# Differential attention written in a fixed, skewed order of units, with output-projection pieces as filling

## The chip, the cores and the metric

One core of one Trainium2 chip. The metric is the device time of one execution in microseconds (us), the median of three runs.

## What is computed

A decoder trunk of two layers on x of 1024 rows by 1024 columns, float32. Each layer first mixes tokens in three groups (a gated convolution A, differential attention B, a chunked gating unit C), projects the joined result with `w_out`, and then runs a convolutional feed-forward part. Shifts, scales and gates ("modulation") come from a conditioning vector through `w_ada`. The part that the change touches is B, here for head h and the 128 query rows of block i (cut from the reference):

```python
for i in range(seq // ATTN_BLOCK):
    q0 = i * ATTN_BLOCK
    end = q0 + ATTN_BLOCK
    qb, kb, vb = q[:, :, :, q0:end], k[:, :, :, :end], v[:, :, :end]   # 2 maps m per head, 64 columns each
    s = jnp.einsum("bhmqd,bhmkd->bhmqk", qb, kb) * scale
    mask = jnp.arange(end)[None, :] <= (q0 + jnp.arange(ATTN_BLOCK))[:, None]
    p = jax.nn.softmax(jnp.where(mask, s, -jnp.inf), axis=-1)
    a = p[:, :, 0] - lam * p[:, :, 1]
    outs.append(jnp.einsum("bhqk,bhke->bhqe", a, vb))
o = rms_norm(concatenate(outs), subln_g) * (1.0 - lam_init)
```

## The kernel before

TensorE (PE) does the matmuls, VectorE (DVE) and ScalarE (ACT) what lies between them, GpSimd (POOL) some of the weight preparation; SyncE (SP) issues all DMAs. Products of float32 precision are three matmuls of split operands: names that end in `h` and `l` are the high and low part of a matrix.

A layer runs in this order. Stage 1 projects the input: the gated convolution, v, the gating unit (stage C, with the tiles `zc`, `uv`, `cvh`, `cvl`, `sv`), then q and k of the heads. The taps of the convolution (`convacc`) and, in layer 0, the modulation (`macc`, `modp`: a weighted sum on DVE of eight `w_ada` tiles, one multiply each, for each of six columns) run beside the projections as background. Then comes attention, then the boundary (matmuls `og`, the rest of the output projection), then the feed-forward part.

Attention has 4 heads of 8 row blocks, 32 units. Block i sees i+1 blocks of keys, so a unit is `w = (i+1)*128` wide. A unit is:

- scores `sc` of maps m=0 and 1 on PE (`score`, L733, on 64 rows each; the mask is added by a matmul, L735). If i >= 4 each map has its own score slot in PSUM of 1024 columns; if i < 4 both share one. There are two slots.
- the maximum `mx` on DVE (one for each map if i >= 4, L754, otherwise one for both, L756), the exponential `p` with its sum on ACT (L759)
- reciprocal, `rho` and the difference of the maps on DVE (L762 to L767)
- transposes `at` on PE (L774) and their copies on ACT (L775), the product with v, `pv`, on PE (L778), its scaling `ot` and sum of squares on ACT (L780, L781)

`head_end` normalises a head, turns it and splits it into `ybh`, `ybL`, which are the left operands of a part of the output projection.

Beside the units runs filling: `out_fill` computes the output projection in pieces of 512 columns, `of`. First 16 pieces over four contraction blocks (12 matmuls each, from `yah`, `ych` and the split weights `woh`, `wol`), then 16 pieces over two blocks (6 matmuls each, from heads 0 and 1). Each ends with a sum into the residual tile `r` on DVE (L862). During attention PSUM holds the two score slots, three banks for `at`, `pv` and the like, and one bank, `fill`, for the pieces and for the key projection of head 3 (`prf`). A scheduler sets the order on each engine: attention is a generator and the pieces are recorded after it, and the scheduler moves them between the units. Weights for the pieces are loaded, multiplied by the gate row on POOL (`scaled_wout`, L682) and split by a copy on ACT and a subtraction (`split_wout`).

In layer 0 the modulation of column 3 runs within attention from head 1 on, one step after each unit; its page holds three raw tiles `wada` and the sum.

Of the kernel before, what the change touches and what calls it, by code (L numbers as in the profile page):

```python
# [50 lines left out]
class Trunk:  # L51
# [575 lines left out]
    def stage1(self, l, H, O, pre):  # L627
# [7 lines left out]
        if l == 0:  # L635
            self.mod_cfg = ("Rb", "Rb")
            self.bg.append(self.mix(self.mods(0, (2, 4)), self.conv_taps(l, self.y[0], self.acc[0], 0)))
        else:
            self.bg.append(self.conv_taps(l, self.y[0], self.acc[0], 0))
# [24 lines left out]
        self.at = O + "c"  # L664
        att = self.attention(l, self.X, O, stk, vp, grow)
        self.qk_head(l, 3, H, O, 0, (0,))
        next(att)
        self.qk_head(l, 3, H, O, 0, (1,), True)
        self.at = self.X + "c"
        return att, grow  # L670
# [66 lines left out]
    def attn_unit(self, l, at, stk, vp, i, ot, ss):  # L737
        nc = self.nc
        w = (i + 1) * P
        small = i < 4  # L740
        sums = self.sm("sums", [P, 2], bufs=4)
        mx = self.sm("mx", [P, 2], bufs=4)
        if small:
            ps2 = self.mm("sc")
            p2 = self.page("tmp", "p")
            ps = [ps2[:, 0:512], ps2[:, 512:1024]]
            pr = [p2[:, 0:512], p2[:, 512:1024]]
        else:
            ps = [self.mm("sc"), self.mm("sc")]
            pr = [self.page("tmp", "p") for _ in range(2)]  # L750
        self.score(ps, stk, i)
        for m in range(2):
            if not small:
                nc.vector.tensor_reduce(out=mx[:, m:m + 1], in_=ps[m][:, :w], axis=AX.X, op=ALU.max, negate=True)  # L754
        if small:
            nc.vector.tensor_reduce(out=mx, in_=ps2.rearrange("p (m k) -> p m k", m=2)[:, :, :w], axis=AX.X,  # L756
                                    op=ALU.max, negate=True)
        for m in range(2):
            nc.scalar.activation(out=pr[m][:, :w], in_=ps[m][:, :w], func=AF.Exp, bias=mx[:, m:m + 1],  # L759
                                 accum_out=sums[:, m:m + 1])  # L760
        rc = self.sm("rc", [P, 2], bufs=4)
# [4 lines left out]
        ad = pr[0]  # L766
        self.unit_end = nc.vector.scalar_tensor_tensor(out=ad[:, :w], in0=pr[1][:, :w], scalar=rho, in1=ad[:, :w],  # L767
                                       op0=ALU.mult, op1=ALU.add)
        a = self.page(at, "at")
        for b0 in range(0, i + 1, 4):  # L770
            b1 = min(i + 1, b0 + 4)
            pb = self.bank("at")
            for j in range(b0, b1):
                nc.tensor.transpose(pb[:, (j - b0) * P:(j - b0 + 1) * P], ad[:, j * P:(j + 1) * P], self.ident)  # L774
            nc.scalar.copy(a[:, b0 * P:b1 * P], pb[:, :(b1 - b0) * P])  # L775
        po = self.bank("pv")
        for j in range(i + 1):
            nc.tensor.matmul(po[:, 0:P], a[:, j * P:(j + 1) * P], vp[:, j, :], start=j == 0, stop=j == i)  # L778
        o = ot[:, i, :]
        nc.scalar.activation(out=o, in_=po[:, 0:P], func=AF.Identity, scale=rc[:, 0:1])  # L780
        nc.scalar.activation(out=po[:, 256:384], in_=o, func=AF.Square, accum_out=ss[:, i:i + 1])  # L781

    def head_end(self, l, h, O, ot, ss, halves=(0, 1)):
# [3 lines left out]
        self.rsqrt(ss[:, cs], ss[:, cs])  # L787
        o = ot[:, cs]
        nc.vector.tensor_tensor(out=o, in0=o, in1=ss[:, cs].unsqueeze(2).to_broadcast([P, 4 * len(halves), P]),
                                op=ALU.mult)  # L790
# [25 lines left out]
    def attention(self, l, H, O, stk, vp, grow):  # L816
        pend = None
        for h in range(4):
            ot = self.page("rows", "ot", shape=(P, NT, P))
            ss = self.sm("oss", [P, NT])  # L820
            for n, i in enumerate((7, 6, 3, 5, 2, 4, 1, 0) if h < 3 else (7, 6, 5, 4, 0, 1, 2, 3)):
                self.attn_unit(l, self.at, stk, vp, i, ot, ss)
                if n == 1 and pend:
                    self.head_end(*pend)
                if h >= 1 and l == 0:
                    if n == 0 and h == 1:
                        self.mod_cfg = (None, None)
                        mt = self.page(H + "a", "wada", shape=(P, 4, 1024))
                        self.mod_tile = [mt[:, i] for i in range(4)]
                        late = self.mods(0, (3,))  # L830
                    with self.tc.issue_after(self.unit_end.ins):
                        next(late, None)
                if n == (1 if h else 4) and h + 1 < 4:
                    nxt = self.load_stacks(l, h + 1, H)
                    nvp = self.load_vp(l, h + 1)
                k = {(2, 3): 0, (2, 5): 1, (2, 7): 2, (3, 0): 3}.get((h, n))
                if k is not None:
                    if k < 2:
                        self.lhs0.append(self.load_yb(l, k, O))
                    self.wB.append(self.load_wout(l, 2 + k, O, grow, self.page(O + "a", "wout")))  # L840
                if h == 3 and n == 4:
                    self.head_end(l, h, O, ot, ss, (1,))
                yield
            pend = (l, h, O, ot, ss)
            stk, vp = nxt, nvp
        self.head_end(*pend, (0,))
        if l == 0:
            for _ in late:
                pass
            self.affine_cols(0, 1)  # L850

    def out_fill(self, lhs, w, r, tiles, scale=1.0):
        nc = self.nc
        for t in tiles:
            ts_ = slice(t * P, (t + 1) * P)
            for n in range(2):
                ns = slice(n * 512, (n + 1) * 512)
                pb = self.bank("of", "fill")
                for k in range(len(lhs)):
                    self.mm3(pb, lhs[k][0][:, ts_], lhs[k][1][:, ts_], w[k][0][:, ns], w[k][1][:, ns], k == 0,  # L860
                             k == len(lhs) - 1)
                nc.vector.scalar_tensor_tensor(out=r[t][:, ns], in0=r[t][:, ns], scalar=scale, in1=pb, op0=ALU.mult,  # L862
                                               op1=ALU.add)
# [26 lines left out]

    def stage3(self, l, H, O, att):
        nc = self.nc
        att, grow = att
        raws = self.page(H + "a", "wout", shape=(P, 4, 1024))
        for i in range(4 - len(self.woA)):
            self.woA.append(self.scaled_wout(l, KA[len(self.woA)], grow, raws[:, i]))
        wA = [self.split_wout(O, raw) for raw in self.woA]
        ab = None
        if l == 0:
            ab = self.page("rows", "ab")  # L900
# [530 lines left out]
```

## Time and profile before

| | before |
|---|---|
| median of three runs | 2440.6 us (2437.98 to 2442.28) |
| profiled execution: time, span | 2437.79 us, 2436.1 us |
| PE, DVE, ACT, POOL busy | 2308.1, 1956.1, 1049.9, 328.9 us |
| granted PE clock, mean | 0.974 |
| attention, layer 0 (286.0 to 507.1) | 221.1 us |
| attention, layer 1 (1492.0 to 1708.2) | 216.2 us |
| stage C to the end of `sv`, layer 0 and 1 | 86.7 and 75.4 us |

The profiled execution is one run of the program; its span ends a little before its time does. Times in the trace count from the start of the span. A matmul's row has a modelled end, so the time that a run of matmuls takes is read from the start of the first to the start of what follows.

### The profile page before, as it was taken

What the parts mean: (1) busy time and instruction counts of PE and PEld (TensorE: products, weight loads), DVE (VectorE), ACT (ScalarE), POOL (GpSimd) and SP (SyncE); (2) the same over time, 40 slices, a digit from 0 to 9 for tenths busy, and PEclk for the clock granted to TensorE, in tenths of its full rate; (3) what the DMA queues carried; (4) which work ended last, traced back from release to release, by engine and by line L of the source; (5) the groups of instructions that cost most, each with busy time, mean ns of one, the idle gap of its engine ahead of it and who ended that gap; (6) DMA issues with size and microseconds to landing.
All of it is one profiled execution on the core that took longest, in us unless ns stands there. A gap on an engine that the chain in (4) does not pass through costs nothing.

```text
span 2436.1 us, 28260 instructions
## 1 busy us (share of the span) xinstructions
PE 2308.1 (95%) x10846; PEld 1886.4 (77%) x10846; DVE 1956.1 (80%) x2650; ACT 1049.9 (43%) x1692; POOL 328.9 (13%) x165
## 2 busy tenths in 40 slices
PE   8998999979999999999959999999899999999996
PEld 7787778767888887788848877777688888878885
DVE  7898876778887888877978988657987777797857
ACT  4214754646554555311130257555654555561111
POOL 1143260410000000000020541214100000000003
PEclk9998999999999999999979999999999999999998
DMA  7433462122332333745523244320232222254301
GB/s 294 156 116 120 140 224 104 61 95 90 110 113 88 112 113 121 263 141 179 190 70 117 78 143 160 130 95 27 99 100 87 78 78 87 87 176 169 122 26 69
DMA packets 87672, 294.06 MB, mean 121 GB/s; under 512 B 9265, under 2 KB 18801, under 8 KB 86001
## 3 DMA queue, kind: packets, MB, share of 16 engines
q1 hardware_dynamic: 87536, 292.26, 35.4%
q8 instruction: 85, 1.39, 0.2%
q14 instruction: 51, 0.41, 0.1%
HBM read 228.23 MB, written 64.00 MB: 120 GB/s over the span
## 4 chain that ended last, share of the span: by engine, by line
PE 67%; DVE 17%; issue 6%; ACT 4%; DMA 3%; POOL 2%; SPq 0%; POOLq 0%; DVEq 0%; ACTq 0%
PE upb L1083 6%; PE upb L1084 6%; PE upb L1085 6%; PE og L130 5%; PE og L131 5%; PE og L132 5%; PE sc L733 3%; PE upd L1084 3%; PE upd L1085 3%; PE upd L1083 3%; DVE convacc L410 2%; PE pv L778 2%; PE of L130 2%; PE of L132 2%; PE of L131 2%
## 5 line engine op out<-in xcount | busy, mean ns | idle before, releaser
L1083 PE MATMUL upb<-comb,uw 128*128 128x512 f32 x704 | 274.9, 391 | 9.9 <-DVE upc L1107 5.0
L130 PE MATMUL og<-dn,dn 128*128 128x512 f32 x704 | 275.3, 391 | 2.6 <-ACT r L885 2.1
L131 PE MATMUL og<-dn,dn 128*128 128x512 f32 x704 | 274.5, 390 | 0.0
L132 PE MATMUL og<-dn,dn 128*128 128x512 f32 x704 | 274.3, 390 | 0.0
L1084 PE MATMUL upb<-comb,uw 128*128 128x512 f32 x704 | 274.0, 389 | 0.0
L1085 PE MATMUL upb<-comb,uw 128*128 128x512 f32 x704 | 273.9, 389 | 0.0
L1107 DVE TENSOR_TENSOR uw<-wu,uw 128x512 fp32r<-128x512 f32 x210 | 144.1, 686 | 125.3 <-ACT uw L1110 125.3
L1120 DVE SCALAR_TENSOR_TENSOR cv<-upc,pc,cv 128x1023 f32<-128x1023 f32 (+1 forms) x176 | 225.4, 1280 | 2.9
L138 POOL TENSOR_TENSOR lnrs<-lnrs,mhalf 128x1 f32<-128x1 f32 x32 | 24.8, 779 | 1421.4 <-DVE lnrs L137 1414.9
L887 DVE TENSOR_TENSOR r<-og,r 128x1024 f32<-128x1024 f32 x128 | 155.7, 1218 | 59.0 <-PE og L132 58.4
L410 DVE SCALAR_TENSOR_TENSOR convacc<-convy,pc,convacc 128x1023 f32<-128x1023 f32 (+14 forms) x120 | 176.2, 1469 | 2.3
L125 ACT CAST dn<-actr 128x1024 fp32r<-128x1024 f32 x44 | 46.1, 1049 | 298.1 <-issue 224.4
L1083 PEld LDWEIGHTS upb<-comb,uw 128*128 128x128 f32 x704 | 132.1, 188 | 41.0 <-DVE upc L1107 6.7
L1110 ACT CAST uw<-wu 128x512 fp32r<-128x512 f32 x210 | 121.7, 616 | 83.6 <-DVE wu L1107 77.1
L130 PEld LDWEIGHTS og<-dn,dn 128*128 128x128 f32 x704 | 132.2, 188 | 31.5 <-ACT r L885 3.4
L1085 PEld LDWEIGHTS upb<-comb,uw 128*128 128x128 f32 x704 | 132.2, 188 | 27.5
L132 PEld LDWEIGHTS og<-dn,dn 128*128 128x128 f32 x704 | 132.2, 188 | 27.4
L1084 PEld LDWEIGHTS upb<-comb,uw 128*128 128x128 f32 x704 | 132.2, 188 | 27.2
L131 PEld LDWEIGHTS og<-dn,dn 128*128 128x128 f32 x704 | 132.2, 188 | 26.8
L1083 PE MATMUL upd<-comb,uw 128*128 128x512 f32 x352 | 137.3, 390 | 0.0
L1085 PE MATMUL upd<-comb,uw 128*128 128x512 f32 x352 | 136.9, 389 | 0.0
L1084 PE MATMUL upd<-comb,uw 128*128 128x512 f32 x352 | 136.9, 389 | 0.0
(312 smaller groups left out, 5474.4 us busy)
## 6 DMA issues: line engine op xcount, KB each, us to landing
wada<-in_w_ada SPq DMA_DIRECT2D x96, 512.0 KB, 4.6
wu<-in_w_up_t SPq DMA_DIRECT2D x84, 512.0 KB, 3.6
d_act<-cv SPq DMA_DIRECT2D x44, 512.0 KB, 2.6
actr<-d_act SPq DMA_DIRECT2D x44, 512.0 KB, 4.6
wdn<-in_w_down SPq DMA_DIRECT2D x44, 512.0 KB, 4.2
win<-in_w_fm SPq DMA_DIRECT2D x24, 512.0 KB, 4.0
wtm<-in_w_tm SPq DMA_DIRECT2D x16, 512.0 KB, 3.7
wout<-in_w_out SPq DMA_DIRECT2D x16, 512.0 KB, 6.2
```

Of the source, the lines that this page charges most:

```text
L130: mm(ps, lh, rh, start=first, stop=False)
L131: mm(ps, lh, rl, start=False, stop=False)
L132: mm(ps, ll, rh, start=False, stop=last)
L410: nc.vector.scalar_tensor_tensor(out=acc[:, d:], in0=y[:, :S - d], scalar=w(30 - d), in1=acc[:, d:], op0=ALU.mult, op1=ALU.add)
L733: nc.tensor.matmul(ps[m][:, c0:c1], q[ms, isl], k[ms, c0:c1], start=n == 0, stop=n == 2 and c1 != w)
L887: nc.vector.tensor_tensor(out=r[t], in0=ps, in1=r[t], op=ALU.add)
L1083: mm(ps, w[:, 0, ks], hi[k], start=k == 0 and not more, stop=False, skip_group_check=True)
L1084: mm(ps, w[:, 0, ks], lo[k], start=False, stop=False, skip_group_check=True)
L1085: mm(ps, w[:, 1, ks], hi[k], start=False, stop=k == 3, skip_group_check=True)
L1107: v.tensor_tensor(out=o, in0=x, in1=y, op=op)
L1110: act.copy(self.up_w[n][:, 0], src)
L1120: v.scalar_tensor_tensor(out=u[:, d:], in0=c[:, :S - d], scalar=self.ffw[:, 2 - d, m:m + 1], in1=u[:, d:], op0=ALU.mult, op1=ALU.add)
```

## The change

Attention no longer depends on the scheduler: it stands in a section in which PE, ACT and DVE keep the order of the code. The unit is cut into `att_score`, `att_max`, `att_exp`, `att_diff`, `att_turn`, `att_copy`, `att_mix` and `att_out`, and three units are in flight: in step g stand the scores, maxima and exponentials of unit g, the difference, transposes and copies of unit g-1, and the product and scaling of unit g-2. `ev` is the residual sum of a filling piece; it is issued one step after its piece, behind the maxima of the next unit.

```diff
-            self.bg.append(self.mix(self.mods(0, (2, 4)), ...))
+            self.bg.append(self.mix(self.mods(0, (2,)), ...))
...
+        with self.tc.manual_schedule(engines={nc.tensor.engine, nc.scalar.engine, nc.vector.engine}):
+            r = self.attention(l, H, self.X, O, stk, vp, grow, wk)
...
+        for g, (h, n, i) in enumerate(units):
...
+            self.att_score(u, stk)
+            if one:
+                self.att_diff(l, one)
+            self.att_max(u)
+            if one:
+                self.att_turn(one)
+            self.att_exp(u)
+            if one:
+                self.att_copy(one, (O if g < 7 else X) + "c")
+            if ev:
+                ev()
+            if two:
+                self.att_mix(two)
+            fills = keys if g < 8 else fillA if g < 22 else fill0
+            ev = next(fills, None) if g < 4 or 10 <= g < 21 or g >= 26 else None
+            if two:
+                self.att_out(two)
...
+            if 10 <= g < 15 or g >= 26:
+                if ev:
+                    ev()
+                ev = next(fills, None)
...
+            k = {4: 0, 5: 1, 8: 2, 9: 3}.get(g)
+            if k is not None:
+                self.wA.append(self.split_wout(O, self.woA[k]))
...
+            if h == 1 and n == 3 and l == 0:
+                self.mod_cfg = (None, None)
+                self.mod_tile = [self.page(X + "c", "wada") for _ in range(2)]
+                late = self.mods(0, (3, 4))
...
+            if g == 21:
...
+                wr = [self.scaled_wout(l, 2 + k, grow, self.page(O + "a", "wout")) for k in range(2)]
+            if g in (23, 24):
...
+                self.wB.append(self.split_wout(O, wr[g - 23]))
+            if g == 25:
+                wr = [self.scaled_wout(l, 4 + k, grow, self.page(O + "a", "wout")) for k in range(2)]
+            if g in (28, 29):
+                self.wB.append(self.split_wout(O, wr[g - 28]))
+            next(late, None)
+            one, two = u, one
```

The blocks of head 0 come in the order 3, 7, 6, 2, 5, 1, 4, 0, of heads 1 and 2 in 7, 6, 3, 5, 2, 4, 1, 0 and of head 3 in 7, 6, 5, 4, 0, 1, 2, 3, as before but for head 0. The key projection of head 3 is cut into four chunks of 12 matmuls for g = 0 to 3 (evacuated on ACT, `evac`, one step after the second and the fourth) and three steps of its rotation. The 16 long pieces stand two in each unit of g = 10 to 14 and one in g = 15 to 20, the short ones two in each unit from g = 26 and four behind the last. `head_end` is cut into `head_norm`, `head_scale` and `head_turn`. The modulation of column 4 moves from stage 1 into attention, behind column 3, and their page has one raw tile and the sum. After the last unit its difference, transposes, product and scaling follow, and the four short pieces, each with its sum.

PE around a unit with i=5 of a later head, before. `sc` with two numbers is a score slot, `of` a piece, `at` and `pv` the transposes and the product with v.

```order
L774 MATMUL at_511_3038<-ident_69,p_506_3012 128x128 x4
L774 MATMUL at_512_3044<-ident_69,p_506_3012 128x128 x4
L733 MATMUL sc_544_3182<-stk_438_2770,stq_437_2768 128x512 x3
L733 MATMUL sc_544_3182<-stk_438_2770,stq_437_2768 128x256 x3
L735 LDWEIGHTS identb_74
L735 MATMUL sc_544_3182<-maskb_76,identb_74 128x128
L130 MATMUL of_717_3935<-woh_315_2320,yah_282_2106 128x512
L131 MATMUL of_717_3935<-wol_316_2321,yah_282_2106 128x512
```

And a unit with i=5 of the changed kernel:

```order
L735 MATMUL sc_427_2741<-stk_367_2514,stq_366_2512 128x256
L735 MATMUL sc_428_2742<-stk_367_2514,stq_366_2512 128x256
L735 MATMUL sc_427_2741<-stk_367_2514,stq_366_2512 128x256
L735 MATMUL sc_428_2742<-stk_367_2514,stq_366_2512 128x256
L737 LDWEIGHTS identb_74
L737 MATMUL sc_427_2741<-maskb_76,identb_74 128x128
L737 LDWEIGHTS identb_74
L737 MATMUL sc_428_2742<-maskb_76,identb_74 128x128
L792 MATMUL at_432_2765<-ident_69,p_420_2690 128x128 x4
L804 MATMUL pv_437_2778<-vp_368_2516,at_422_2694 128x128 x7
L131 MATMUL of_438_2786<-woh_341_2418,yah_272_2071 128x512
L132 MATMUL of_438_2786<-wol_342_2419,yah_272_2071 128x512
```

Before, the slot of one map is filled alone, with a piece behind it; now the two slots alternate, and transposes, product and piece stand behind both.

DVE in layer 0 before, where a head's units with i=7 and i=6 follow each other (`r` is the residual tile that a piece is summed into):

```order
L764 TENSOR_SCALAR rho_509_3034<-rc_508_3032,sums_502_3008,nlam0_103 128x1
L862 SCALAR_TENSOR_TENSOR r_385_2569<-r_385_2569,of_715_3907 128x512
L767 SCALAR_TENSOR_TENSOR p_506_3012<-p_507_3013,rho_509_3034,p_506_3012 128x1024
L754 TENSOR_REDUCE mx_516_3072<-sc_517_3073 128x1
L754 TENSOR_REDUCE mx_516_3072<-sc_518_3074 128x1
L862 SCALAR_TENSOR_TENSOR r_395_2602<-r_395_2602,of_716_3921 128x512
```

And in the changed kernel, for two units with i >= 4:

```order
L748 TENSOR_REDUCE mx_502_3126<-sc_498_3105 128x1
L748 TENSOR_REDUCE mx_502_3126<-sc_499_3106 128x1
L917 SCALAR_TENSOR_TENSOR r_458_2903<-r_458_2903,of_495_3086 128x512
L261 SCALAR_TENSOR_TENSOR wada_442_2820<-wada_441_2819,cact_85,wada_442_2820 128x1024
L777 RECIPROCAL rc_512_3175<-sums_506_3133 128x2
L779 TENSOR_SCALAR rho_513_3177<-rc_512_3175,sums_506_3133,nlam0_103 128x1
L782 SCALAR_TENSOR_TENSOR p_504_3131<-p_505_3132,rho_513_3177,p_504_3131 128x1024
L748 TENSOR_REDUCE mx_514_3180<-sc_510_3159 128x1
L748 TENSOR_REDUCE mx_514_3180<-sc_511_3160 128x1
L917 SCALAR_TENSOR_TENSOR r_458_2903<-r_458_2903,of_509_3142 128x512
```

The sum of a piece now always stands behind both maxima of the next unit, and a multiply of the modulation (`wada`) behind the sum.

DVE in stage C of layer 0 before, with the taps of the convolution and the multiplies of the modulation:

```order
L410 SCALAR_TENSOR_TENSOR convacc_150_1095<-convy_149_1093,pc0_89,convacc_150_1095 128x1003
L260 SCALAR_TENSOR_TENSOR macc_131_876<-wada_139_950,cact_85,macc_131_876 128x1024
L137 TENSOR_SCALAR crs_189_1362<-cmv_187_1356 128x2
L410 SCALAR_TENSOR_TENSOR convacc_150_1095<-convy_149_1093,pc0_89,convacc_150_1095 128x1002
L555 TENSOR_TENSOR zc_191_1423<-ptm_190_1374,brow_155_1109 128x1024
L260 SCALAR_TENSOR_TENSOR macc_131_876<-wada_140_954,cact_85,macc_131_876 128x1024
```

And DVE at the same taps in the changed kernel:

```order
L411 SCALAR_TENSOR_TENSOR convacc_140_1060<-convy_139_1058,pc0_89,convacc_140_1060 128x1002
L138 TENSOR_SCALAR crs_179_1327<-cmv_177_1321 128x2
L411 SCALAR_TENSOR_TENSOR convacc_140_1060<-convy_139_1058,pc0_89,convacc_140_1060 128x1001
L570 TENSOR_SCALAR uv_176_1319<-uv_176_1319,cmv_177_1321,crs_179_1327 128x256 x2
L411 SCALAR_TENSOR_TENSOR convacc_140_1060<-convy_139_1058,pc0_89,convacc_140_1060 128x1000
```

The multiplies (`macc`) between the taps are gone there.

More of the change, by code (lines that the diff above doesn't have):

```diff
@@ L747, in attn_unit @@
-            pr = [p2[:, 0:512], p2[:, 512:1024]]
-        else:
-            ps = [self.mm("sc"), self.mm("sc")]
-            pr = [self.page("tmp", "p") for _ in range(2)]
-        self.score(ps, stk, i)
+            pr = u["p"] = [p2[:, 0:512], p2[:, 512:1024]]
+        else:
+            pr = u["p"] = [self.page("tmp", "p") for _ in range(2)]
+        sums = u["sums"] = self.sm("sums", [P, 2], bufs=4)
         for m in range(2):
-            if not small:
-                nc.vector.tensor_reduce(out=mx[:, m:m + 1], in_=ps[m][:, :w], axis=AX.X, op=ALU.max, negate=True)
@@ L755, in attn_unit, with att_diff @@
[L755 to L759, printed above, removed]
+            nc.scalar.activation(out=pr[m][:, :w], in_=u["ps"][m][:, :w], func=AF.Exp, bias=u["mx"][:, m:m + 1],
                                  accum_out=sums[:, m:m + 1])
[L761 removed]
+    def att_diff(self, l, u):
+        nc = self.nc
+        w, sums = u["w"], u["sums"]
+        rc = u["rc"] = self.sm("rc", [P, 2], bufs=4)
@@ L765, in attn_unit, with att_turn @@
                                 op1=ALU.mult)
[L766 to L769, printed above, removed]
+        ad = u["p"][0]
+        nc.vector.scalar_tensor_tensor(out=ad[:, :w], in0=u["p"][1][:, :w], scalar=rho, in1=ad[:, :w], op0=ALU.mult,
+                                       op1=ALU.add)
+    def att_turn(self, u):
+        i, ad = u["i"], u["p"][0]
+        u["pb"] = []
         for b0 in range(0, i + 1, 4):
@@ L814, in load_yb @@
         return hi, lo
[L816 to L846, printed above, removed]
@@ new lines, in key_chunks, with evac @@
+    def key_chunks(self, l, h, H, w):
+        nc = self.nc
+        m = ZT["k"] + h
+        hi, lo = w
+        bias = self.col(l, "bin", m)
+        z, rot = self.page("raw", "z"), self.page("Rb", "rot")
+        for half in range(2):
+            sl = slice(half * 512, (half + 1) * 512)
+            pb = self.bank("prf", "fill")
+            for k in range(KT):
+                ks = slice(k * P, (k + 1) * P)
+                self.mm3(pb, hi[:, ks], lo[:, ks], H[0][k][:, sl], H[1][k][:, sl], k == 0, k == KT - 1)
+                if k == 3:
+                    yield
+            def evac(sl=sl, pb=pb):
+                nc.scalar.activation(out=z[:, sl], in_=pb, func=AF.Identity, bias=bias)
+                self.rotate(rot[:, sl], pb, bias, 1.0)
+            yield evac
+        nc.vector.tensor_tensor(out=z, in0=z, in1=self.trig[0], op=ALU.mult)
+        yield
+        nc.vector.tensor_tensor(out=rot, in0=rot, in1=self.trig[1], op=ALU.mult)
+        yield
+        nc.vector.tensor_tensor(out=z, in0=z, in1=rot, op=ALU.add)
+        nc.scalar.copy(rot.bitcast(F32R), z)
+        nc.vector.tensor_tensor(out=z, in0=z, in1=rot, op=ALU.subtract)
+        for x, t in enumerate((rot, z)):
+            nc.sync.dma_start(self.d_k[l][h, :, x, :], t)
+        yield
@@ L889, in out_group @@
                 after(t)
[L891 to L900, printed above, removed]
-            nc.sync.dma_start(ab, self.gab(0, 0, 1))
-        order = (4, 5, 0, 1, 2, 3, 6, 7)
-        r = {}
-        for t in order:
-            next(att)
-            r[t] = self.load_res(t, ab)
-        for _ in att:
-            pass
-        self.out_fill(self.lhsA, wA, r, order, 1.0 if l else ALPHA)
-        self.out_fill(self.lhs0, self.wB[:2], r, order)
-        self.psum(3, 2)
-        self.up_first(l, O + "c")
-        return r, self.lhsB, self.wB[2:]
     def boundary(self, l, w, lhs, wts, r, X):
```

176 lines of the change are left out of this document (138 added, 38 removed).

## The prediction

> **What bounds the kernel now.** I read the share of each engine first, then the busy time in stretches (each layer's attention whole, then the four heads of layer 1), then the waits in that window.
>
> ```profile
> PE 2308.1 (95%) x10846; PEld 1886.4 (77%) x10846; DVE 1956.1 (80%) x2650; ACT 1049.9 (43%) x1692; POOL 328.9 (13%) x165
> ```
> ```profile
> core 0: us, PE busy (x) PEld busy (x) DVE busy (x) ACT busy (x) POOL busy (x), PEclk, DMA share, GB/s
> 286.00:507.10 221.10, 206.52 (x1170) 162.89 (x1170) 156.71 (x221) 125.07 (x317) 75.32 (x31) 0.95 0.33 115
> 1492.00:1708.20 216.20, 202.89 (x1153) 158.80 (x1153) 141.83 (x210) 124.96 (x318) 54.20 (x23) 0.97 0.27 98
> ...
> 1492.00:1549.00 57.00, 49.41 (x245) 37.42 (x244) 41.78 (x47) 42.40 (x80) 21.75 (x8) 0.88 0.58 216
> 1549.00:1601.00 52.00, 52.00 (x303) 41.03 (x303) 27.81 (x47) 23.46 (x70) 1.65 (x1) 1.00 0.15 52
> 1601.00:1647.00 46.00, 46.00 (x288) 37.33 (x287) 27.08 (x42) 26.14 (x74) 8.79 (x5) 1.00 0.28 97
> 1647.00:1708.00 61.00, 55.28 (x321) 42.84 (x321) 45.11 (x74) 32.83 (x95) 22.03 (x10) 1.00 0.09 27
> ```
> The kernel is bound by PE. Attention, which the change rewrites, takes 221.1 and 216.2 us. In heads 1 and 2 of layer 1 PE is never idle, while DVE is busy 53% and 59% of the time: whatever order the scheduler found there, it hides every maximum, exponential and residual sum under matmuls. Slack lies only in head 0 (7.6 us idle, clock 0.88) and at the end of head 3.
>
> ```profile
> PE of L130 <- DVE r L862: 5.2, 6, 1.8
> PE of L132 <- POOL yal L126: 3.6, 1, 3.6
> PE sc L733 <- ACT rot L380: 2.9, 1, 2.9
> PE sc L733 <- ACT p L759: 0.8, 2, 0.4
> ```
> So PE waits hardly at all for softmax (0.8 us), and for the sum of the previous filling piece six times. That wait exists because all pieces share one bank: the next one starts when the sum L862 has read the last. A new order can gain what PE does needlessly, and can lose all of this cover.
>
> **What PE does needlessly.** The rows below are PE in head 1 of layer 1.
>
> ```profile
> 1558.37 1.50 PE L733 MATMUL sc<-stk,stq 64*128 64x512 f32 x6
> 1559.80 0.23 PE L735 MATMUL sc<-maskb,identb 128*128 128x128 bf16 x1
> 1559.84 0.48 PE L130 MATMUL of<-woh,yah 128*128 128x512 f32 x1
> ...
> 1562.66 0.60 PE L778 MATMUL pv<-vp,at 128*128 128x128 f32 x4
> 1563.10 0.27 PE L774 MATMUL at<-ident,p 128*128 128x128 f32 x1
> 1563.30 0.97 PE L733 MATMUL sc<-stk,stq 64*128 64x512 f32 x6
> 1564.21 0.28 PE L735 MATMUL sc<-maskb,identb 128*128 128x128 bf16 x2
> ```
> Six score matmuls of one map, each on 64 rows, start over 1559.80 - 1558.37 = 1.43 us. Six of a small unit, whose two maps alternate on rows 0-63 and 64-127, take 1564.21 - 1563.30 = 0.91. The new order alternates in large units too. For i=7 (12 of these and 12 slots of 512 in two maps) the score falls from 2 x 1.43 to 2 x 0.91 us. With the narrower second halves in proportion, I estimate S = 1.8, 1.65, 1.5 and 1.4 us for i = 7, 6, 5, 4, against 3.0, 2.6, 2.3 and 2.2: 3.8 us a head, 15 us a layer. For i = 3, 2, 1, 0 S is about 1.1, 0.95, 0.8 and 0.75, as before. That is the only work saved.
>
> **What the order puts in the path.** Unit g now issues on PE: score(g), transposes of g-1, product with v of g-2, one filling piece; on DVE: difference of g-1, maxima of g, sum of the *previous* piece. The piece must wait for that sum, the sum stands behind both maxima, the maxima wait for the whole alternating score.
>
> ```profile
> L754 DVE TENSOR_REDUCE mx<-sc 128x1 f32<-128x1024 f32 x8 | 9.8, 1219 | 6.0 <-PE sc L735 6.0
> ...
> L754 DVE TENSOR_REDUCE mx<-sc 128x1 f32<-128x896 f32 x8 | 8.6, 1088 | 5.0 <-PE sc L735 5.0
> ...
> L759 ACT ACTIVATE p<-sc,mx 128x1024 f32<-128x1024 f32 x8 | 8.9, 1118 | 7.3 <-DVE mx L754 7.3
> ...
> L754 DVE TENSOR_REDUCE mx<-sc 128x1 f32<-128x768 f32 x8 | 7.6, 953 | 1.3 <-PE sc L735 1.2
> ...
> L754 DVE TENSOR_REDUCE mx<-sc 128x1 f32<-128x640 f32 x8 | 6.6, 822 | 6.8 <-PE sc L735 6.5
> ...
> L767 DVE SCALAR_TENSOR_TENSOR p<-p,rho,p 128x1024 f32<-128x1024 f32 x4 | 6.0, 1509 | 0.1
> ```
> ```profile
> 1696.97 0.50 PE L130 MATMUL of<-woh,ybh 128*128 128x512 f32 x1 [1.83 <-DVE r L862]
> ...
> 1698.23 0.39 PE L132 MATMUL of<-woh,ybL 128*128 128x512 f32 x1
> 1698.66 0.69 DVE L862 SCALAR_TENSOR_TENSOR r<-r,of 128x512 f32<-128x512 f32 x1 [1.06 <-PE of L132]
> ...
> 1699.40 0.19 PEld L130 LDWEIGHTS of<-woh,ybh 128*128 128x128 f32 x1 [1.21 <-DVE r L862]
> ```
> The second fence is the wait itself: 1.83 us where a normalisation stood before the sum on DVE; then last start at 1698.23, sum at 1698.66 for 0.69, next piece at 1699.40. From the last start that is 1.17 us, 0.94 of it without a start. A piece of twelve matmuls is 1562.66 - 1559.84 = 2.8 us, one of six 1.45.
>
> One piece in a large unit: S + two maxima + sum 0.69 + hand-overs 0.3 + piece 2.8. For i = 7, 6, 5, 4: 1.8 + 2.44 + 3.8 = 8.0; 7.6; 7.2; 6.8. Between score and piece PE has only the transposes and the product, about 0.11 us a matmul (the row of four at 1562.66 lasts to 1563.10): i=7 has 3.4 us to cover and 1.7 us of work, so 1.7 idle in each. A small unit has one maximum over both maps (1.22, 0.95, 0.69, 0.42 by the rows of the same widths, the last three estimated in proportion): i = 3, 2: 6.1, 5.6 us.
>
> Two pieces: add 0.94 + 2.8 (or 0.94 + 1.45). No piece: the next large unit needs both score slots, so it waits for the second exponential: S + two maxima + exponential 1.1 + 0.3: 5.7 for i=7, 5.2 for i=6; i = 4, 1, 0 give about 4.2, 3, 2.6.
>
> Now by head, layer 1. Head 0 has no output pieces, the key projection in their place, which must be evacuated from that bank by ACT; I take 57, as now (my bounds are 52 and 62: its two pieces, 5.7 us, leave it, and an evacuation on ACT stands ahead of the second half). Head 1: two units without piece, five with two long ones (i = 3, 5, 2, 4, 1), one with one: 5.7 + 5.2 + (9.8 + 10.9 + 9.3 + 10.5 + 9.0) + 5 = 65, against 52. Head 2: five units with one piece, three without: 8.0 + 7.6 + 6.1 + 7.2 + 5.6 + 9.8 = 44, against 46. Head 3: two without, six with two short pieces, then four short ones that have nothing but the sums beside them, and the last unit's way through difference (1.5 at most), transposes, copy, product and evacuation, 4.8 in all by my estimate: 10.9 + (8.2 + 7.8 + 6 + 6.3 + 6.7 + 7.2) + 4 x 2.44 + 4.8 = 68, against 61. In all +13 -2 +7 = +18 a layer, although PE does 15 us less. I use it for layer 0 too; the 5 us by which that is longer now stay in it. The split of `head_end` in three is costed at nothing: the same instructions, beside pieces that PE runs for 2.8 us; without that cover they would cost their 0.7 to 1.3 us each.
>
> Weight copies: `wout` loads at g=21 are scaled on POOL and copied by ACT at g=23 and 24, in its queue ahead of the next copies and exponentials. From load to scaled copy go 6.2 + 2.76 us, g=22 and 23 are about 6 us long.
>
> ```profile
> L682 POOL TENSOR_TENSOR wout<-wout,grow 128x1024 f32<-128x1024 f32 x6 | 16.5, 2763 | 19.5 <-DMA wout<-in_w_out 19.4 <-PE sc L735 0.2
> ```
> ```profile
> wada<-in_w_ada SPq DMA_DIRECT2D x96, 512.0 KB, 4.6
> ...
> wout<-in_w_out SPq DMA_DIRECT2D x16, 512.0 KB, 6.2
> ```
> I add 4 us a layer for it (0 to 8). Those at g=8, 9, 28 and 29 are older when copied: nothing.
>
> **Layer 0: the modulation.** Eight multiplies leave stage 1 and join eight others in attention, one per unit from g=11, with one raw page instead of three: each load starts after the multiply before it.
>
> ```profile
> L260 DVE SCALAR_TENSOR_TENSOR macc<-wada,cact,macc x7: 1272/1274/2308, 175.9 to 199.0; 128x1024 f32<-128x1024 f32 x7
> L258 DVE TENSOR_SCALAR macc<-wada,cact x1: 710/710/710, 172.8 to 172.8; 128x1024 f32<-128x1024 f32 x1
> ```
> ```profile
> 139.20:225.90 86.70, 79.66 (x347) 64.99 (x345) 83.75 (x106) 18.40 (x20) 34.33 (x16) 0.92 0.30 99
> 1357.10:1432.50 75.40, 71.67 (x328) 59.39 (x326) 70.76 (x90) 18.71 (x21) 37.19 (x17) 0.98 0.19 60
> ```
> The last two rows are the same place (stage C) in layers 0 and 1: DVE is busy 97% of it in layer 0, and layer 1, which has no multiplies there, is 11.3 us shorter. I take 9 us back (0 to 11). In attention a multiply can come no faster than 4.6 + 1.28 = 5.9 us after the last, and DVE, in order, stands in front of it with the next difference and maximum behind. Where a unit is longer it fits beside the piece; g=21 to 25 (4.2, 3, 2.6, 5.7, 5.2) would be drawn out to 5.9: +9. The loads on SP now also hold back the `yb` and `wout` loads of g=21: +2. Stacks and v of the next head are issued seven units ahead: nothing.
>
> **The clock.** These are windows of four microseconds in layer 1.
>
> ```profile
> 1496.00:1500.00 4.00, 3.38 (x15) 2.45 (x14) 2.26 (x1) 3.95 (x5) 3.90 (x2) 1.00 0.44 149
> 1500.00:1504.00 4.00, 1.75 (x4) 1.46 (x5) 2.71 (x3) 3.94 (x4) 0.59 (x1) 0.73 0.00 0
> 1504.00:1508.00 4.00, 3.56 (x10) 2.25 (x9) 3.98 (x2) 3.95 (x7) 1.77 (x1) 0.50 0.00 0
> ...
> 1694.00:1698.00 4.00, 2.17 (x9) 1.43 (x9) 3.56 (x8) 0.94 (x3) 0.26 (x1) 1.00 0.00 0
> ```
> PE busy 1.75 of 4 us: the clock goes to 0.50 for the next window and longer. Busy 2.17 of 4, with the gap of 1.83 us shown above: it stays 1.00. The new order's gaps lie about there: 1.7 in units with a piece, 2.3 or more in those without, in the key evacuation and in the tail. I take three such stretches more in a layer, of 6.8 us, that cost half of it: +10 a layer (0 to +28). [...] Here 1.75 us of work in 4 was already too little.
>
> **Sum.** Layer 1: 18 + 4 + 10 = +32. Layer 0: 18 + 4 + 11 + 10 - 9 = +34. Against the profiled execution's 2437.8 us that is 2504; the median of the runs is 2.8 higher, so 2505.
>
> **Rivals.**
> A, without the clock: the order waits as above but PE keeps 1.00. The kept clock in the window from 1694 speaks for it. 2505 - 20 = 2485. Chance 0.24.
> B, the clock falls again and again: ten stretches a layer, since the gaps repeat in each unit: +28 instead of +10: 2541. The three windows from 1496 speak for it; against it, that most gaps are cut in two by the product. Chance 0.13.
> C, faster: the sums don't hold PE. If DVE reaches the sum while PE still has transposes and product to do, the piece starts at once, units are PE's own work and the 15 us a layer come through, with the 9 of stage 1: 2440.6 - 30 - 9 = 2402. It decides at i=7: S to piece must shrink from 3.4 us to the 1.7 of PE work, that is, the sum must run before the maxima. That DVE is busy only 53% in head 1 speaks for it; against it, that DVE works strictly down its own list, with the sum behind both. Chance 0.12.
> D, the gains and waits cancel, 2436 to 2445: 0.03.
> My own case keeps 0.48, from 2490 to 2530.
>
> **Range and chances.** 2435 to 2550 leaves out C and the upper part of B. About 0.2% (5 us) is what a measurement of this kernel can tell from no change: faster 0.12, same 0.03, slower 0.85.
>
> **What would show it.** Right: score groups of i=7 in 1.8 us; PE waits for the sum in nearly every filled unit, over 30 us a layer instead of 5; head 1 of layer 1 near 65 us, and PE idle in it; stage C of layer 0 near 77 us; DVE waiting for `wada` around g=21; clock under 0.97. Wrong: if PE stays busy through heads 1 and 2, C holds; if waits are there but heads shorter than 60, my hand-overs or maxima are too dear; if head 0 is far from 57, the key projection's evacuation was mis-sized.

## The result and the profile after

The changed kernel takes 2534.6 us (2531.1 to 2537.2) against 2440.9: ratio 1.0381, 95% interval 1.0366 to 1.0397. It is slower by 94 us; forecast were 64, with a range to 2550.

The share of each engine, then the stretches of the changed kernel that answer to those shown of before (attention of both layers, heads of layer 1, stage C of layer 0):

```profile
PE 2306.6 (91%) x10846; PEld 1881.0 (74%) x10846; DVE 1944.4 (77%) x2650; ACT 1052.4 (42%) x1692; POOL 327.5 (13%) x165
```
```profile
277.00:558.70 281.70, 209.73 (x1186) 163.63 (x1185) 160.50 (x230) 126.55 (x317) 75.91 (x31) 0.85 0.30 105
1543.30:1804.40 261.10, 200.95 (x1153) 155.02 (x1153) 140.16 (x211) 125.88 (x316) 51.94 (x23) 0.88 0.22 79
...
1543.30:1609.60 66.30, 41.37 (x232) 32.34 (x231) 34.13 (x45) 41.56 (x83) 15.03 (x6) 0.79 0.39 145
1609.60:1677.90 68.30, 59.53 (x343) 46.45 (x342) 30.39 (x49) 26.35 (x75) 6.39 (x3) 0.96 0.22 77
1677.90:1724.20 46.30, 39.62 (x265) 31.43 (x264) 25.39 (x44) 22.95 (x67) 2.82 (x2) 0.96 0.25 91
1724.20:1804.40 80.20, 60.42 (x316) 44.81 (x316) 50.25 (x74) 35.02 (x91) 27.71 (x13) 0.84 0.07 20
...
140.60:216.36 75.76, 71.37 (x331) 58.66 (x329) 71.49 (x94) 18.51 (x20) 35.72 (x16) 1.00 0.17 56
```
The columns are the stretch and its length, busy time of PE, PE's weight loads, DVE, ACT and POOL, then the granted clock. Attention grew by 60.6 and 44.9 us, stage C shrank by 10.9; together +94.6. DVE, ACT and POOL have the work of before. In layer 1 PE is idle for 261.1 - 200.95 = 60 us, where it was 13. Its busy time is nearly unchanged (201.0 for 202.9), although alternating scores save PE some 19 us (the run map by map below): by the estimate under "The clock" below, up to 17 of these go to the lower clock. The granted clock is either 1.00 or 0.50 here, so a mean of 0.88 over 261 us means some 62 us at half rate, against 14 before (0.97 over 216). In layer 0 it is 0.85, some 83 us, against 20.

One unit with i=7 and one piece, in head 2 of layer 1:

```profile
1677.94 1.66 PE L735 MATMUL sc<-stk,stq 64*128 64x512 f32 x12
1679.53 0.29 PE L737 MATMUL sc<-maskb,identb 128*128 128x128 bf16 x2
1679.65 0.28 PE L792 MATMUL at<-ident,p 128*128 128x128 f32 x1
1679.77 0.61 PE L804 MATMUL pv<-vp,at 128*128 128x128 f32 x4
1679.80 2.36 DVE L748 TENSOR_REDUCE mx<-sc 128x1 f32<-128x1024 f32 x2 [3.70 <-PE sc L737]
...
1682.07 0.68 DVE L917 SCALAR_TENSOR_TENSOR r<-r,of 128x512 f32<-128x512 f32 x1
...
1682.80 0.50 PE L131 MATMUL of<-woh,yah 128*128 128x512 f32 x1 [2.42 <-DVE r L917]
1683.14 0.39 PE L132 MATMUL of<-wol,yah 128*128 128x512 f32 x1
...
1685.04 0.63 PE L132 MATMUL of<-wol,ych 128*128 128x512 f32 x1
1685.47 0.63 PE L133 MATMUL of<-woh,ycl 128*128 128x512 f32 x1
```
Here is the predicted chain: score in 1.7 us (to 1679.65), two maxima, the sum behind them, the piece behind the sum. PE stands still for 2.42 us. Then comes what the sum of the prediction was too small for: the piece starts at full clock, and from about 1684 its matmuls follow each other every 0.43 us instead of 0.23.

PE's waits in attention of layer 1:

```profile
PE at L792 <- DVE p L782: 17.6, 7, 7.8
PE of L131 <- DVE r L938: 9.6, 10, 2.4
PE sc L735 <- ACT p L770: 7.7, 7, 2.0
PE of L131 <- DVE r L917: 7.6, 8, 2.4
PE prf L131 <- ACT rot L381: 5.9, 1, 5.9
PE sc L735 <- ACT rot L381: 4.7, 1, 4.7
PE of L131 <- DVE r L990: 3.3, 1, 3.3
PE of L131 <- DVE r L992: 1.6, 2, 0.8
```
The sums (four rows, `r`) hold PE for 22 us; in the kernel before it was 5.2. The sum that stands behind the maxima (L917) is 7.6 of these, the second sum of units with two pieces (L938) 9.6, the tail the rest. Another 17.6 go to transposes that wait for a difference, 11.9 of them in head 0, and 5.9 to the evacuation of the key projection in head 0.

### The profile page after: what moved, and what is told of

It is laid out like the page before. It is cut to its first block, busy times and chain, and to the rows that moved or that the text cites. A ratio compares the mean times of both kernels' runs of the same rounds, so it can differ in the third digit from the quotient of the medians.

```text
span 2535.4 us, 28238 instructions
## 1 busy us (share of the span) xinstructions
PE 2306.6 (91%) x10846; PEld 1881.0 (74%) x10846; DVE 1944.4 (77%) x2650; ACT 1052.4 (42%) x1692; POOL 327.5 (13%) x165
## 4 chain that ended last, share of the span: by engine, by line
PE 61%; DVE 15%; ACT 4%; issue 4%; POOL 2%; DMA 1%; DVEq 0%; POOLq 0%; ACTq 0%
PE upb L1208 6%; PE upb L1209 6%; PE upb L1210 6%; PE og L131 5%; PE og L133 5%; PE og L132 5%; PE upd L1208 3%; PE upd L1209 3%; PE upd L1210 3%; PE of L131 2%; PE of L133 2%; PE of L132 2%; PE sc L735 2%; PE upa L1208 1%; PE upa L1210 1%
## 5 line engine op out<-in xcount | busy, mean ns | idle before, releaser
L770 ACT ACTIVATE p<-sc,mx 128x512 f32<-128x512 f32 (+7 forms) x128 | 93.9, 737 | 231.0 <-DVE mx L744 127.2
L1208 PE MATMUL upd<-comb,uw 128*128 128x512 f32 x352 | 137.1, 390 | 0.0
L1210 PE MATMUL upd<-comb,uw 128*128 128x512 f32 x352 | 137.0, 389 | 0.0
```

Of the source, the lines that this page charges most:

```text
L770: nc.scalar.activation(out=pr[m][:, :w], in_=u["ps"][m][:, :w], func=AF.Exp, bias=u["mx"][:, m:m + 1], accum_out=sums[:, m:m + 1])
L1208: mm(ps, w[:, 0, ks], hi[k], start=k == 0 and not more, stop=False, skip_group_check=True)
L1210: mm(ps, w[:, 1, ks], hi[k], start=False, stop=k == 3, skip_group_check=True)
```

## The experiments

Each edit is to the changed kernel if nothing else is said, and each time compared with its 2534.6 us is a median; ratios are to the kernel before. In a row for a stretch, which is of one execution, the columns are as above.

**Sums ahead of maxima.**

```diff
             if one:
                 self.att_diff(l, one)
+            if ev and g >= 8:
+                ev()
+                ev = None
             self.att_max(u)
```


> The changed kernel with one edit: from step 8 on, the sum of the previous piece is issued on DVE ahead of the maxima of the unit, not behind them. Theory (the order holds the piece back behind both maxima): PE's waits of a piece for the sum, 20.7 us in layer 0 and 20.5 us in layer 1, fall to under 8 us each, and with them some half clock; the time falls by 20 to 35 us, to 2500 to 2515 us. Rival (the chain score, maxima, exponential, next score is the bound, and the sum was only the last to be seen): the maxima start 0.7 us later, the wait moves from the piece to the next score, and the time stays within 8 us of 2534.6 us, or rises.

Measured: 2517.6 us, ratio 1.0311 (1.0294 to 1.0329): 17 less. Layer 1:

```profile
1535.90:1785.70 249.80, 198.48 (x1154) 155.03 (x1153) 141.07 (x211) 125.78 (x317) 51.90 (x23) 0.88 0.23 83
```
The stretch is 11 us shorter and the waits for the first sum of a unit (7.6 us) are gone, but the second sum in units with two pieces still costs 9.4, and the clock is as low as before. The direction is the theory's, the size is short of its 20 to 35, and 14.3 us of waits for sums are left where it said under 8. What was won is about the wait that was taken away (7.6 us in layer 1, 7.9 in layer 0).

**Scores map by map.**

```diff
+        if i >= 4:
+            for m in range(2):
+                ...   # all segments and products of map m, then its mask
+            return
```


> The changed kernel with one edit: in units with i of 4 or more the score of map 0 is done whole, then that of map 1, as the scheduler had it before; PE does its score in twice the time again. Theory (attention is held by waits, so the work that alternating saves on PE is worth nothing there; and map 0's maximum can start earlier): scores take about 62 us a layer from start to start instead of 45, PE's waits shrink by as much, half clock gets rarer, and the time is 2505 to 2535 us. Rival (the saving of 15 us a layer is real and only covered by the waits): 2560 to 2570 us.

Measured: 2547.9 us, ratio 1.0432 (1.0414 to 1.0451): 13 more. Neither theory holds as it stood. Layer 0, then layer 1:

```profile
273.80:563.10 289.30, 233.08 (x1185) 182.30 (x1185) 161.48 (x230) 127.68 (x317) 74.09 (x31) 0.86 0.30 102
1545.80:1809.10 263.30, 219.98 (x1153) 170.34 (x1152) 139.98 (x211) 127.61 (x317) 50.97 (x23) 0.90 0.22 78
```
PE is busy 23 and 19 us longer, the stretches are 7.6 and 2.2 us longer. How that falls to the layers is rough: this execution is the fastest of the four (2540.0), and layer 1 of the same program took 261.1 us in one execution and 254.3 in another (the run with the modulation back, below). By the medians 13 of the 42 us count. So alternating is worth something, but in the changed kernel most of the time that it saves turns into idle time of PE.

**More for PE to do, behind every product.**

```diff
+        for _ in range(12):
+            self.nc.tensor.matmul(po[:, 128:256], self.identb, self.maskb, start=True, stop=True)
```


> The changed kernel with one addition: after each product with v, twelve matmuls of 128 columns into a part of that bank that nobody reads. They add only work for PE, in front of the piece that waits. Theory (the clock, halved after idle stretches, is 15 to 20 us of each layer's loss): the half clock in attention falls from 62 and 83 us to under 30 us each, and the time falls by 10 to 30 us although PE does more. Rival (the clock follows but the waits set the units): no half clock saved in the units' chain, and the added matmuls cost up to 12 x 0.06 us x 62 units = 45 us where PE wasn't waiting: 2535 to 2580 us.

Measured: 2545.7 us, ratio 1.0432 (1.0406 to 1.0459): 11 more.

```profile
1552.50:1819.20 266.70, 219.23 (x1538) 176.25 (x1537) 140.85 (x211) 126.73 (x317) 51.87 (x23) 0.89 0.22 78
```
The clock went from 0.88 to 0.89 only: PE got 18 us of work in 32 units, 0.6 in each, and that does not fill the places where it stands for two to eight. The theory failed in its form, and the time is in the rival's range; on what the clock costs this run says nothing.

**Product ahead of transposes.**

```diff
             self.att_max(u)
+            if two:
+                self.att_mix(two)
             if one:
                 self.att_turn(one)
...
-            if two:
-                self.att_mix(two)
```


> The changed kernel with one edit: on PE the product with v of unit g-2 stands ahead of the transposes of unit g-1 instead of behind them. Theory (transposes wait for the difference on DVE, 28.2 us in layer 0 and 17.6 us in layer 1, with the product idle behind them though its operands are there): that wait falls by 8 to 12 us a layer, the time to 2510 to 2525 us. Rival (the wait is of the single long kind, 4 to 8 us behind the key evacuation and the modulation, against which one product of 0.9 us does nothing, or the product itself waits for the copies on ACT): within 8 us of 2534.6 us.

Measured: 2514.0 us, ratio 1.0304 (1.0283 to 1.0325): 20.5 less. PE's waits in layer 1, first four:

```profile
PE of L131 <- DVE r L938: 9.4, 10, 2.4
PE of L131 <- DVE r L919: 8.2, 8, 2.4
PE sc L735 <- ACT p L770: 7.2, 9, 2.0
PE at L792 <- DVE p L782: 6.1, 3, 3.4
```
The wait of the transposes fell from 17.6 to 6.1 us, and in layer 0 from 28.2 to 18.9. The theory holds: a product that was ready stood behind transposes that were not.

**Head 0.** The evacuation of the key projection ahead of the exponentials, and a step between the rotation's copy and its subtraction.

```diff
+            if ev and g < 8:
+                ev()
+                ev = None
             self.att_exp(u)
...
-            if 4 <= g < 7:
+            if 4 <= g < 8:
...
         nc.scalar.copy(rot.bitcast(F32R), z)
+        yield
         nc.vector.tensor_tensor(out=z, in0=z, in1=rot, op=ALU.subtract)
```


> The changed kernel with two edits in head 0: the key projection is evacuated on ACT ahead of the unit's exponentials instead of behind its copies, and the subtraction that ends the key's rotation stands one step behind the copy that it waits for instead of right behind it on DVE. Theory (head 0 grew from 55.5 to 66.3 us in layer 1 because PE waits there once 5.9 us for the evacuation and once 7.8 us for a difference that stands behind the subtraction): head 0 falls by 5 to 9 us in each layer and the time by 10 to 18 us. Rival (the exponentials, now behind 3.5 us of evacuation on ACT, are late instead): head 0 within 3 us, the time within 8 us of 2534.6 us.

Measured: 2514.0 us, ratio 1.0293 (1.0276 to 1.0310): 20.5 less. Head 0 of layer 1, and its whole attention:

```profile
1530.10:1584.30 54.20, 38.31 (x232) 30.06 (x231) 37.74 (x45) 42.26 (x84) 16.32 (x6) 0.85 0.44 157
1530.10:1779.90 249.80, 199.62 (x1153) 154.40 (x1153) 144.13 (x211) 126.59 (x317) 53.20 (x23) 0.89 0.24 83
```
Head 0 takes 54 us instead of 66, not more than in the kernel before. Theory shown, and more than it asked. How much each of the two edits does isn't separated.

**All three together.** No new lines.

> The changed kernel with three reorderings at once: sums ahead of maxima, product ahead of transposes, and the two edits of head 0. Apart, the first two took off 17 and 20.5 us. Theory (waits at different places of a unit): the gains nearly add, 2470 to 2490 us, PE's idle time in attention falls to 35 to 45 us a layer. Rival (they take turns at the same wait): 2500 to 2512 us.

Measured: 2483.0 us, ratio 1.0168 (1.0152 to 1.0184): 52 less, where the three apart gave 58. Layer 0, then layer 1:

```profile
274.00:534.50 260.50, 210.22 (x1185) 164.21 (x1185) 167.11 (x230) 126.33 (x317) 77.39 (x31) 0.85 0.33 114
1520.20:1749.90 229.70, 191.28 (x1153) 148.94 (x1153) 143.05 (x211) 125.56 (x316) 53.90 (x23) 0.93 0.26 90
```
They nearly add. PE's idle time in layer 1 falls from 60 to 38 us and the clock rises to 0.93; in layer 0 it falls from 72 to 50, and the clock stays at 0.85. More than half of the change's loss was the order within a unit and in head 0.

**The modulation back in stage 1.**

```diff
-  self.mods(0, (2,))      ...  late = self.mods(0, (3, 4))
+  self.mods(0, (2, 4))    ...  late = self.mods(0, (3,))
```


> The changed kernel with the modulation of column 4 back in stage 1 of layer 0; in attention only column 3 is left, one step a unit from step 11, still with one raw page. Theory (the move is worth about what it costs: -9 in stage C, +11 in attention by the prediction; the trace of the changed kernel has -11 in stage C, while attention of layer 0 is 20.5 us longer than of layer 1, against 4.8 before): stage C goes back to 87 us, attention of layer 0 falls by 10 to 16 us to 266 to 272, and the total is 2526 to 2537 us. Rival (the loads that the multiplies wait for are the reason that layer 0 lost 60 us and layer 1 only 45): attention falls by over 18 us and the total is under 2526 us.

Measured: 2522.6 us, ratio 1.0329 (1.0313 to 1.0344): 12 less. Attention of layer 0, stage C, and attention of layer 1:

```profile
284.00:549.80 265.80, 202.76 (x1169) 157.34 (x1169) 153.66 (x221) 126.51 (x317) 74.00 (x31) 0.88 0.27 95
138.20:224.00 85.80, 77.14 (x343) 63.02 (x341) 82.81 (x102) 18.38 (x19) 34.12 (x16) 0.92 0.30 97
...
1534.40:1788.70 254.30, 197.50 (x1153) 152.78 (x1153) 140.01 (x211) 126.01 (x317) 51.93 (x23) 0.90 0.23 81
```
Attention of layer 0 falls by 15.9 us, as the theory has it, and stage C grows by 10; the end of layer 0's attention comes 8.9 us earlier. The total is where the rival has it, but part of that isn't the modulation's: layer 1, whose program this edit leaves alone, is 6.8 us shorter in this execution than in that of the changed kernel. So differences of some 7 us between single stretches show little. DVE waited for `wada` five times in the changed kernel, 8.6 us in all (first row, of layer 0). After the longest of these waits the multiply took 3.09 us, and both held a difference and with it PE for 7 us:

```profile
DVE wada L261 <- DMA wada<-in_w_ada: 8.6, 5, 4.4
```
```profile
464.93 3.09 DVE L261 SCALAR_TENSOR_TENSOR wada<-wada,cact,wada 128x1024 f32<-128x1024 f32 x1 [4.42 <-DMA wada<-in_w_ada]
...
469.07 0.66 PE L792 MATMUL at<-ident,p 128*128 128x128 f32 x2 [6.97 <-DVE p L782]
```

**The modulation alone, in the kernel before.**

```diff
-  self.mods(0, (2, 4))    ...  late = self.mods(0, (3,))
+  self.mods(0, (2,))      ...  late = self.mods(0, (3, 4))
```


> The kernel before with the modulation part of the change alone: column 4 moves from stage 1 into attention, behind column 3, with the three raw pages and the scheduler's order kept. Theory (stage C is bound by DVE, attention isn't): stage C shortens by 9 to 11 us, attention of layer 0 grows by 0 to 4, the total is 2431 to 2437 us. Rival (the multiplies cost the same wherever they stand): within 4 us of 2441 us.

Measured: 2448.3 us, ratio 1.0034 (1.0022 to 1.0047): slower by about 7, which neither theory had.

```profile
275.80:515.20 239.40, 220.67 (x1185) 173.12 (x1185) 168.32 (x233) 125.11 (x317) 76.66 (x31) 0.89 0.35 123
136.10:215.80 79.70, 73.76 (x330) 60.83 (x329) 74.70 (x95) 18.78 (x20) 35.79 (x16) 0.95 0.20 68
```
Stage C is 7 us shorter, but attention takes 239.4 us instead of 221.1, with the clock at 0.89 instead of 0.95, though three raw pages and the scheduler were kept. PE is idle only 4 us longer there; it is busy 14 us longer. Three of the eight multiplies, from 437.92 us on, took 3.4 us each instead of 1.28, while POOL prepared weights, and from 436.6 to 463.9 us the clock was half. Behind the second of them the maxima were late, and PE waited for the exponential:

```profile
443.59 3.38 DVE L260 SCALAR_TENSOR_TENSOR wada<-wada,cact 128x1024 f32<-128x1024 f32 x1
...
446.89 2.34 DVE L754 TENSOR_REDUCE mx<-sc 128x1 f32<-128x1024 f32 x2
...
449.40 0.79 PE L733 MATMUL sc<-stk,stq 64*128 64x512 f32 x1 [3.35 <-ACT p L759]
```
So these eight multiplies cost more inside attention than in stage C, where DVE is busy 97% of the time (83.75 of 86.70 us). Whether the scheduler's order of the rest has a part in it isn't separated.

**The piece ahead of the transposes**, with the three reorderings and the modulation back.

```diff
             if two:
                 self.att_mix(two)
+            if 10 <= g < 21 or g >= 26:
+                ev = next(fills, None)
             if one:
                 self.att_turn(one)
```


> The changed kernel with all reorderings so far (sums ahead of maxima, product ahead of transposes, the two edits of head 0), the modulation of column 4 back in stage 1, and one more: a unit's piece stands ahead of the transposes on PE, and in units with two pieces the transposes stand between them, so that they cover the sum that the second piece waits for. Theory (what is left in head 1 and 3 is that sum, 11.3 us in layer 1, and the difference that the transposes wait for): layer 1's attention falls from 229.7 to 212 to 222 us, layer 0's to 225 to 240, and the time to 2438 to 2460 us. Rival (transposes behind the piece make the copies on ACT late, and the next product waits for them): layer 1 stays over 225 us, the time over 2460 us.

Measured: 2480.1 us, ratio 1.0154 (1.0132 to 1.0177); layer 1 takes 233.3 us. The rival's times hold; its reason doesn't show, since PE waits for the copies 1.9 us in layer 1, and 1.6 in the run of the three.

**The same with scores map by map.**

> The same order as the run before it, with the scores of large units done map by map again. Theory (work that PE saves counts as far as PE no longer waits; in the changed kernel alternating was worth 12 us of the 50 that the scores differ by): with most waits gone it is worth more, so this kernel is 20 to 35 us slower than its twin. Rival (the units are held by the chain maxima, exponential, next score, and map 0's earlier maximum makes up for the work): within 10 us of its twin.

Measured: 2497.9 us, ratio 1.0231 (1.0211 to 1.0251): 18 slower than its twin, between theory and rival. Layer 1 of the two, the twin first:

```profile
1517.10:1750.40 233.30, 197.24 (x1154) 153.66 (x1153) 143.83 (x211) 127.21 (x317) 53.53 (x23) 0.90 0.26 88
```
```profile
1526.80:1769.80 243.00, 216.15 (x1154) 167.62 (x1153) 142.81 (x211) 128.44 (x317) 52.71 (x23) 0.91 0.24 85
```
PE does 18.9 us more here and the layer takes 9.7 more. In both layers PE's work is again some 42 us: 18 of them count by the medians, with the changed order 13.

**The four without that piece order**, that is, the three reorderings with the modulation back.

> The three reorderings (sums ahead of maxima, product ahead of transposes, head 0) with the modulation of column 4 back in stage 1, and the pieces behind the transposes. Theory (the modulation costs 12 us where it was moved to, whatever the order; the piece ahead of the transposes, tried with the same rest, cost as much as it gained): 2466 to 2476 us, layer 1 as in the run of the three, 230 us. Rival (with fewer waits the multiplies hide in attention): 2480 us or more. Against the kernel before neither reaches 2441.

Measured: 2480.0 us (2473 to 2485), ratio 1.0158 (1.0137 to 1.0179). It is not distinguishable from the piece ahead of the transposes, nor from the three alone. With the three in place the 12 us of the modulation no longer show in the medians (3 us, in runs that spread over 12); why is open.

**Idle matmuls where PE waits long.**

```diff
+            if g in (5, 7):
+                self.warm(self.bank("warm", "fill"), 16 if g == 5 else 34)
             if one:
                 self.att_turn(one)
...
+        dm = self.mm("warm")
+        self.warm(dm, 14)
         for ev in fill0:
+            self.warm(dm, 3)
             ev()
```


> The changed kernel with idle matmuls only where PE waits long: 64 and 136 of 128 columns in steps 5 and 7 ahead of the transposes that wait 3.8 and 7.8 us (layer 1), 56 in the tail ahead of the second short piece and 12 behind each piece there. They write where nobody reads. Theory (a stretch of half clock follows each long wait and slows the work behind it): the half clock of attention falls from 62 us in layer 1 and 83 in layer 0 by 15 us or more each, and since PE works at half rate for some 5 to 9 us of that, the time falls by 6 to 16 us. Rival (what runs in those stretches isn't what the next step waits for): the half clock falls, the time stays within 4 us of 2534.6 us.

Measured: 2529.2 us, ratio 1.0355 (1.0341 to 1.0370): 5.4 less by the medians, between theory and rival.

```profile
1544.40:1798.60 254.20, 209.34 (x1446) 166.12 (x1445) 139.75 (x211) 126.40 (x317) 51.89 (x23) 0.93 0.23 81
...
1592.78 5.03 PE L816 MATMUL warm<-maskb,identb 128*128 128x128 bf16 x64 [3.78 <-ACT rot L381]
```
In layer 1 the clock rises from 0.88 to 0.93, some 25 us less at half rate, and the stretch is 6.9 us shorter although PE was given work. In layer 0 neither moved enough to tell. This does not price the half clock. Layer 1 took 254.3 us without any idle matmuls too, in the run with the modulation back. And the edit does not do all that it was meant to: the 64 idle matmuls of step 5 write into the bank `fill`, so they waited for its evacuation themselves (the row at 1592.78) and then stood for 5 us in front of the transposes.

None of the versions reaches the kernel before: the best are 1.5% slower. So some 54 of the 94 us are won back by edits; the other 40 no run takes apart.

## Why the prediction was right

- **PE as the bound, waits as the price.** Right. The score of i=7 takes 1.7 us as forecast, and most of the saving vanishes: with the scores undone PE works 42 us longer, and the kernel loses only 13. The 0.3 us for hand-overs in a unit were an estimate; the unit at 1677.94 has 0.23 (4.86 us to its piece, less 1.59 of score matmuls, 2.36 of maxima and 0.68 of sum).

  The sum comes out 30 us short. Layer 1 grew by 45 us instead of 32, attention of layer 0 by 61 instead of 43 (18 + 4 + 11 + 10). The result lies above the 2530 us at which the prediction's own case ends, and below rival B's 2541. It is inside the range because that had room for B's clock, but a good part of what filled the room is head 0, the transposes and `head_end`, named below, which the sum had at nothing or not at all. That the total fits is partly luck. (The last step of the sum is 2 us off: 2503.8 and 2.8 make 2506.6.)
- **The sum behind both maxima.** Right in mechanism: 22 us of waits a layer instead of 5, less than the 30 named. Of these only 7.6 are the sum behind the maxima; 9.6 are ten second pieces, most of them 0.8 where 0.94 was forecast. Moving the first sum alone gave 17 us in both layers.
- **The heads.** Layer 1: forecast 57, 65, 44, 68, measured 66, 68, 46, 80, with the clock and the weight copies in them, for which the prediction added 14. Heads 1 and 2 are within 4 us by the unit formula. Head 0 failed: "I take 57, as now" was mis-sized by 9. The bounds named the evacuation on ACT, not the subtraction on DVE behind an ACT copy; the head 0 run shows that the two cost 12 us in layer 1. In head 3 the formula took undisturbed durations, and "The split of `head_end` in three is costed at nothing" failed. `ybL` of head 2 stands on DVE ahead of the sum and waits 3.43 us for ACT; PE waits for the sum 2.38 us, and its next matmuls, every 0.43 us, run at half clock:

```profile
1760.05 1.41 DVE L840 SCALAR_TENSOR_TENSOR ybL<-obt,subs,ybh 128x512 fp32r<-128x512 f32 x2 [3.43 <-ACT ybh L838]
...
1762.11 0.59 PE L131 MATMUL of<-woh,ybh 128*128 128x512 f32 x1 [2.38 <-DVE r L938]
```
The same happens in the tail, where the sum L990 is late for head 3's `ybL` and normalisation and PE waits 3.3 us, with half clock behind it (0.50 from 1793.1 us on). No run moved `head_end`, so what it costs in all is open.
- **The step that was missing.** The prediction let PE do transposes and product while it waited. It didn't see that the transposes themselves wait for the difference, with the product behind them: 17.6 and 28.2 us; the reordering took 20.5 off the total. Of the 17.6, 11.9 belong to head 0.
- **The modulation.** Stage C: 9 forecast, 10.9 measured. Attention: "+11" was too little; undoing it gave 15.9. The net of +2 was in fact a loss of 9 by the traces up to the end of layer 0's attention, and 12 by the medians.
- **The clock.** "+10 a layer" supposed three more stretches of 6.8 us. Layer 1 has nine stretches at half clock instead of two, 62.5 us instead of 13.7; layer 0 has twelve instead of three. That is the count of rival B. The sums over layer 1's stretches, the changed kernel first, then before:

```profile
sum 62.49, PE 47.18 PEld 35.58 DVE 32.54 ACT 26.38 POOL 15.91; mean PE 5.24 PEld 3.95 DVE 3.62 ACT 2.93 POOL 1.77
```
```profile
sum 13.65, PE 12.31 PEld 9.25 DVE 11.31 ACT 11.46 POOL 5.77; mean PE 6.15 PEld 4.62 DVE 5.65 ACT 5.73 POOL 2.89
```
PE works 47 us in them, 35 more than before. Matmuls of a piece follow each other every 0.43 us there and every 0.23 at full clock. If all that work took half as long at full clock, the clock would by this estimate cost layer 1 at most 17 of its 45 us. How much less it is, no run shows.

The gaps were taken too short as well: "1.7 us of work" behind the score of i=7 counts this unit's own transposes and product, but there stand those of the two small units before it, 0.6 us, and PE is idle 2.42 us instead of 1.7. Rival A, that short gaps keep the clock, is refuted by the row at 1682.80: a gap of 2.42 us, and half clock a microsecond later (from 1683.87 us on).
- **Late weight copies.** Priced at 4 us for the copies on ACT. In layer 1 both take 1.04 us and the exponentials behind them wait for maxima, not for them. What the preparation of these weights costs there shows on DVE: POOL's subtraction for the first stands beside the difference at 1730.23 (last section), and the transposes behind it wait 2.1 us. No run took the copies away. Open.

## What to carry to other kernels

A hand-laid order must be read as the chain that each engine makes of it. Here a short evacuation that frees a shared buffer, put ahead of the long reductions, took off 17 us, and what was ready, put ahead of what still waited, 20.5. Work saved on the busiest engine is worth only the share that does not turn into waits, here 13 of 42 us in one order and 18 of 42 in another. Before moving work out of a stage where an engine is nearly full (DVE 97% in stage C), price it where it lands: in attention three of eight multiplies took 3.4 us instead of 1.28, with a chain of dependent steps behind them.

## What was not expected of the hardware

The same difference (`p`, 1024 wide) takes 1.28 us in one unit and 3.25 in another, where POOL subtracts in the same time:

```profile
1730.04 2.37 POOL L127 TENSOR_TENSOR wol<-wout,woh 128x1024 fp32r<-128x1024 f32 x1
...
1730.23 3.25 DVE L782 SCALAR_TENSOR_TENSOR p<-p,rho,p 128x1024 f32<-128x1024 f32 x1
```
On DVE's bound chain of an i=7 unit that is 2 us. The difference ends 1.07 us after POOL's operation (1733.48 against 1732.41). The trace has more of this. Of DVE's operations of this kind with 1024 columns (`p`, `wada`, `macc`) in the changed kernel, 67 overlap no operation of POOL and take 1.27 to 1.29 us. Eight began while POOL ran one of 1024 columns; they took 1.37 to 3.25 us, and each ended 1.08 to 1.09 us after POOL's. The three multiplies of 3.4 us in the kernel before with the modulation moved show the same. So DVE seems to wait here until POOL is done; no run took POOL's work away to prove it.
